# Product-key top-k of a mixture layer: the gather block's first level moved behind the gate build, softmax exponential ahead of the index decoding

## Chip, cores and metric

One core of one Trainium2 chip runs the whole kernel in one launch. The metric is the device time of one execution in microseconds (us); the kernel is run several times and the median is taken.

## What is computed

A hybrid decoder layer for 512 tokens of width 1024: latent attention and retention side by side, one output projection, then a product-key mixture (PEER) with 128 x 128 experts, each a single neuron, and a final norm. The change lies in the mixture alone. Cut to it, the reference is:

```python
q = (xt @ w_query).reshape(T, 8, 2, 128)               # 8 heads, 2 halves
s = einsum('thpd,pkd->thpk', q, sub_keys)              # 128 scores per half
s_top, i_top = top_k(s, 16)                            # first level
cand = s_top[:, :, 0, :, None] + s_top[:, :, 1, None]  # 16 x 16 sums
best, pos = top_k(cand.reshape(T, 8, 256), 16)         # second level
eidx = take(i_top[:, :, 0] * 128 + i_top[:, :, 1], pos)
g = softmax(best)                                      # gates, 16 a head
a = gelu(einsum('thkd,td->thk', expert_u[eidx], x))
out = einsum('thk,thkd->td', g * a, expert_v[eidx])
```

So every token takes 8 x 16 = 128 experts out of 16384.

## The kernel before

The 512 tokens are four blocks of 128. Blocks 0 to 2 (`DB`) are computed densely: a gate matrix with one column for every expert, mostly zeros, multiplies the activations of all experts. The experts come in 128 chunks of 128. For each chunk c a **U chunk** (`u_chunk`, L782) loads `raw` (L779, on the SP queue), splits it into a high part on ACT (L78) and a low part on POOL for the first 12 chunks and on DVE for the rest (L79), does 24 matmuls of 384 columns (L83 to L85), and applies Gelu on ACT (L794) into a buffer `ga` or `gb`. A **V chunk** (`v_load` L851, `v_mm` L872) loads `vraw` (L857), splits it on ACT and POOL into `vhi` and `vlo`, multiplies the activations with the gates (`wf`, L866; rounded copies `wh` L868 on ACT and `wl` L869 on DVE) and does 18 matmuls of 512 columns. `R0` is 36: 36 U chunks run ahead, so the V loop (L962) does V chunk c and U chunk c + 36 in each round. There are 37 activation buffers; chunk c + 37 takes that of chunk c, which is freed by `wf` of c. `raw` has three buffers, `vraw`, `hi`, `lo`, `vhi`, `vlo`, `wf`, `wh` and `wl` two each, the gates `gtl` three.

Block 3 (`GB`) is computed by gathers: 128 indirect transfers (L883, issued by POOL) fetch the chosen rows of the U table, DVE takes the dot products (L891), and 128 more fetch rows of the V table, which DVE sums (L904). They need the expert indices `eidx`, and run beside the dense loops of V and U chunks.

**Queries and top-k.** `query` (L554) computes, for groups of blocks and heads, the queries, and `scores` (L561) the 128 scores of each half, which ACT copies out of PSUM (L567) into the block's score tile `blk`. `Q0` and `Q1` do heads 0 and 1 of blocks 0, 1 and 2, 3; `Q2` and `Q3` heads 2 to 7 of all four. Behind each head, `level1` (L616) calls `topk16` for each half. It is eight values at a time on DVE:

```python
V.max(vals[:, 0:8], src)                              # L601
V.max_index(idx[:, 0:8], vals[:, 0:8], src)           # L602
V.match_replace(src, vals[:, 0:8], src, -BIG)         # L603
V.max(vals[:, 8:16], src)                             # L604
V.max_index(idx[:, 8:16], vals[:, 8:16], src)         # L605
```

The values of blocks 0 and 1 go to a tile `fhi`, of block 2 to `flo`, of block 3 to `v`. `level2` (L637) forms the 50 sums of a head that can be among the best 16 (L645 to L651) and calls `topk16` on them; it is called for half of the heads at a time, for blocks 0 to 2 first in the middle of the queries. `topk` (L655) decodes the positions into the two index halves with comparisons and trees of additions on DVE (L660 to L690), and takes the best value off the scores (L687 to L689). `gates` (L693) applies Exp on ACT (L697), normalises on DVE, splits the gates of blocks 0 to 2 into a high and a low half (L708 to L710), and for block 3 writes `eidx` (L704, L705). `topk_fin` (L712) transposes a block's indices and gates on TensorE (L717) and copies them to half precision on ACT (L721); it may not be issued ahead of the matmuls of the last U chunk written before it. How many those are by blocks 0, 1 and 2 is the table `UF`.

**Gate build.** `g_steps` (L812) has 48 steps, spread over the U chunks up to the 32nd. Each makes four one-hot arrays on DVE (L823 to L826, three buffers `ohs`), 16 short matmuls (L832, L833), ACT copies into `stg` (two buffers, L836), and a transfer to the gate matrix `Gd` in DRAM (L840), from which the V loop loads it (`gtl`, L848). The last one-hot is kept as `last["o"]`, and the last four U chunks ahead of the V loop are held until it is issued. The memory of the one-hots and of `stg` is that of the front stage, which holds the score tiles of blocks 0 to 2.

**Start of the gathers.** In round `LEAD` = 2 of the V loop (L963), not to be issued ahead of `last["o"]`, come the second level, decoding and gates of block 3. Then `h2n` is loaded (L972), the normalised input of block 3, into memory that was the top-k stage's, and from there on POOL runs in the order in which the program is written: the split `vlo` of a V chunk, then the gathers of that round (2.56 a round on average, later 1.12), beginning with round 2.

What sets the order on the other engines is a scheduler: it goes through the program, and puts instructions that it holds ready ahead of others that wait; within an engine the order is then fixed. Up to L771 the SP queue is by hand, behind it the scheduler's too.

Of the kernel before, what the change touches and what calls it, by code (L numbers as in the profile page):

```python
# [8 lines left out]
F32 = mybir.dt.float32  # L9
# [5 lines left out]
AF = mybir.ActivationFunctionType  # L15
# [6 lines left out]
H = 8  # L22
# [7 lines left out]
GB = 3  # L30
# [6 lines left out]
GPU = 2  # L37
HOLD = 4
NPL = 12
UF = {0: 2, 1: 7, 2: 12}  # L40
QS = (((0, 1), (0, 1)), ((2, 3), (0, 1)), ((0, 1, 2, 3), (2, 3, 4)), ((0, 1, 2, 3), (5, 6, 7)))
LEAD = 2
GSC = float(2 ** 14)
# [7 lines left out]
def build(ctx: ExitStack, tc: tile.TileContext, A, out):  # L51
    nc = tc.nc
    V, S, P, T, G = nc.vector, nc.scalar, nc.gpsimd, nc.tensor, nc.sync
# [6 lines left out]
    def acc():  # L60
        return ps.tile([128, 512], F32, name="acc", bufs=3)

    def tpb():
        return ps.tile([128, 512], F32, name="tp", bufs=2)

    def ab():
        return ps.tile([128, 512], F32, name="ab", bufs=2)
# [4 lines left out]
    def raw_t():  # L72
        return st.tile([128, 1024], F32, name="raw", bufs=3)
# [15 lines left out]
    tk = ptk.enter_context(tc.tile_pool(name="topk", bufs=1, side="right", reuse_waits="tile"))  # L89
# [20 lines left out]
    for hf in range(2):  # L110
        p = tpb()
# [442 lines left out]
    def query(bs, hs):  # L554
        n = len(bs) * 128
        for b in bs:
            Sc[b] = blk[b].rearrange("p a c -> p (a c)").rearrange("p (h q k) -> p h q k", h=8, q=2)
        pend = []

        def scores():  # L560
            qs, h, q = pend.pop()  # L561
            p4 = acc()
            for i in range(len(bs)):
                cs = slice(i * 128, (i + 1) * 128)
                T.matmul(p4[:, cs], qs[:, cs], subk[:, q, :], start=True, stop=True)
            for i, b in enumerate(bs):
                last["qa"] = S.activation(Sc[b][:, h, q], p4[:, i * 128:(i + 1) * 128], AF.Copy).ins  # L567
            if q:
                for b in bs:
                    level1(b, h)  # L570
                if h == H // 2 - 1:
                    for b in DB:
                        level2(b, 0)

        for h in hs:
            for q in range(2):
                raw = raw_t()
                G.dma_start(raw, A["w_query"][2 * h + q])
                hi, lo = split(raw, P)
                pa = ab()  # L580
                for k in range(8):
                    ks = slice(k * 128, (k + 1) * 128)
                    mm3(pa[:, :n], hi[:, ks], lo[:, ks], hh[:, bs[0]:bs[0] + len(bs), k, :],
                        hl[:, bs[0]:bs[0] + len(bs), k, :], k == 0, k == 7)
                qs = w2()
                S.activation(qs[:, :n], pa[:, :n], AF.Copy)
                if pend:
                    scores()
                pend.append((qs, h, q))
        scores()  # L590
# [23 lines left out]
    lv, tin = {}, {}  # L614

    def level1(b, h):  # L616
        if b not in lv:
            if b == 1:
                t = lv[0][2]
            else:  # L620
                t = (tk if b == GB else fr).tile([128, 512 if b == GB else 1024], F32,
                                                 name=("fhi", None, "flo", "v1")[b], bufs=1)
            o = 512 * (b == 1)
            v = t[:, o:o + 256].rearrange("p (h q a) -> p h q a", h=8, q=2)
            i = t[:, o + 256:o + 512].bitcast(U32).rearrange("p (h q a) -> p h q a", h=8, q=2)
            lv[b] = v, i, t
        v1, i1, _ = lv[b]
        for q in range(2):
            topk16(v1[:, h, q, :], i1[:, h, q, :], Sc[b][:, h, q, :], 128)

    def spare(b):
        f = blk[b].rearrange("p a c -> p (a c)")
        return (f[:, 0:128].rearrange("p (h k) -> p h k", h=8),
                f[:, 128:256].bitcast(U32).rearrange("p (h k) -> p h k", h=8),
                f[:, 256:256 + H * NC_].rearrange("p (h n) -> p h n", h=8), f[:, 1024:1536])
# [17 lines left out]
            topk16(bst[:, h], bpos[:, h], cd[:, h], NC_)  # L653

    def topk(b):  # L655
        bst, bpos, _, ti = spare(b)
        i1 = lv[b][1]
        di = tk.tile([128, 2, 17, 8], F16, name="di", bufs=1)
        V.memset(di[:, :, 0, :], 0.0)
        V.tensor_copy(di[:, :, 1:, :], i1.rearrange("p h q a -> p q a h"))  # L660
        dd = tk.tile([128, 2, 16, 8], F16, name="dd", bufs=1)
        V.tensor_sub(dd, di[:, :, 1:, :], di[:, :, :16, :])
        ij = tk.tile([128, 2, 16, 8], F16, name="ij", bufs=1)
        ph = tk.tile([128, 16, 8], F16, name="ph", bufs=1)
        V.tensor_copy(ph, bpos.rearrange("p h k -> p k h"))
        full = [128, 16, 16, 8]

        def t4k():
            return tk.tile([128, 16, 16, 8], F16, name="t4k", bufs=2)

        ge, tm = t4k(), t4k()
        V.tensor_tensor(ge, ph[:, None].to_broadcast(full), kc[:, 0, :, None, :].to_broadcast(full), op=OP.is_ge)
        V.tensor_mul(tm, ge, dd[:, 0, :, None, :].to_broadcast(full))
        tree(ij[:, 0], tm, V)
        V.tensor_mul(ge, ge, kc[:, 1, :, None, :].to_broadcast(full))
        pb = tk.tile([128, 16, 8], F16, name="pb", bufs=1)
        tree(pb, ge, V)
        V.tensor_sub(pb, ph, pb)
        tm = t4k()
        V.tensor_tensor(tm, pb[:, None].to_broadcast(full), kc[:, 2, :, None, :].to_broadcast(full), op=OP.is_ge)  # L680
        V.tensor_mul(tm, tm, dd[:, 1, :, None, :].to_broadcast(full))
        tree(ij[:, 1], tm, V)
        if b == 2:
            ti = tk.tile([128, 512], F32, name="t4k", bufs=2)
        ti = ti.rearrange("p (q s) -> p q s", q=4)
        nm = tk.tile([128, 8], F32, name="nmx", bufs=1)
        V.tensor_copy(nm, bst[:, :, 0])  # L687
        ee = ti[:, 3].rearrange("p (h k) -> p h k", h=8)
        V.tensor_sub(ee, bst, nm[:, :, None].to_broadcast([128, 8, 16]))  # L689
        V.tensor_copy(ti[:, :2], ij.rearrange("p q k h -> p q (k h)"))  # L690
        tin[b] = ti

    def gates(b, after=None):  # L693
        ti = tin[b]
        ee = ti[:, 3].rearrange("p (h k) -> p h k", h=8)
        with tc.issue_after(after) if after else ExitStack():
            S.activation(ee, ee, AF.Exp)  # L697
        se = tk.tile([128, 8], F32, name="se", bufs=1)
        V.reduce_sum(se, ee, axis=AX.X)
        V.reciprocal(se, se)  # L700
        gg = gsm if b == GB else ti[:, 2]
        V.tensor_mul(gg.rearrange("p (k h) -> p h k", h=8), ee, se[:, :, None].to_broadcast([128, 8, 16]))
        if b == GB:
            V.scalar_tensor_tensor(ti[:, 2], ti[:, 0], 128.0, ti[:, 1], op0=OP.mult, op1=OP.add)  # L704
            V.tensor_copy(eidx, ti[:, 2])  # L705
            return
        gh = tk.tile([128, 16, 8], F16, name="pb", bufs=1).rearrange("p k h -> p (k h)")
        V.tensor_scalar(gh, gg, GSC, None, op0=OP.mult)  # L708
        V.scalar_tensor_tensor(ti[:, 3], gg, GSC, gh, op0=OP.mult, op1=OP.subtract)
        V.tensor_copy(ti[:, 2], gh)  # L710
# [16 lines left out]
    last = {}  # L727
# [69 lines left out]
    nu = 0  # L797
    for b in DB:
        level2(b, 1)
        topk(b)  # L800
        gates(b, last["qa"])
        while nu < UF[b]:
            u_chunk(nu, P if nu < NPL else V)
            nu += 1
        topk_fin(b, last["u"])
# [156 lines left out]
    for c in range(NK - LB):  # L962
        if c == LEAD:  # L963
            with tc.issue_after(last["o"]):
                level2(GB, 0)
                level2(GB, 1)
                topk(GB)
                gates(GB)
            ptk.close()
            lg = ctx.enter_context(tc.tile_pool(name="gside", bufs=1, side="right", reuse_waits="tile"))  # L970
            h2n = lg.tile([128, 1024], F32, name="h2n")
            G.dma_start(h2n, h2d)  # L972
            asl = lg.tile([128, 128], F32, name="asl")
            wsl = lg.tile([128, 128], F32, name="wsl")
            ga_it = gather_steps(h2n, asl, wsl)
            ctx.enter_context(tc.manual_schedule(engines={mybir.EngineType.Pool}))
        w = v_load(c)
        for d in range(ND):
            v_mm(c, w, d)
        if c + R0 < NK:  # L980
            u_chunk(c + R0, V)
        if c < LEAD:
            continue
        credit += CR[0] if c + R0 < NK else CR[1]
        while credit >= 1:
            credit -= 1
            next(ga_it, None)
# [89 lines left out]
```

## Time and profile before

| | us |
|---|---|
| median of 3 runs | 1591.3 |
| lowest, highest | 1589.39, 1597.22 |
| the profiled execution | 1585.5 |
| its span | 1583.7 |
| PE (TensorE) busy | 1507.8, 95% |
| DVE busy | 1276.3, 81% |
| POOL busy | 824.2, 52% |
| ACT busy | 622.1, 39% |

The span is what the profiler saw, from the first instruction to the last; the execution's own time is a little longer. Busy times are of one engine each and overlap. PE is the TensorE matmul queue; SP is the queue that issues most transfers. PEclk is the share of full clock that TensorE was granted. In a timeline, "x2" means two instructions put together in a row, and a bracket tells how long the engine was idle before and what ended that.

### The profile page before, as it was taken

What the parts mean: (1) busy time and instruction counts of PE and PEld (TensorE: products, weight loads), DVE (VectorE), ACT (ScalarE), POOL (GpSimd) and SP (SyncE); (2) the same over time, 40 slices, a digit from 0 to 9 for tenths busy, and PEclk for the clock granted to TensorE, in tenths of its full rate; (3) what the DMA queues carried; (4) which work ended last, traced back from release to release, by engine and by line L of the source; (5) the groups of instructions that cost most, each with busy time, mean ns of one, the idle gap of its engine ahead of it and who ended that gap; (6) DMA issues with size and microseconds to landing.
All of it is one profiled execution on the core that took longest, in us unless ns stands there. A gap on an engine that the chain in (4) does not pass through costs nothing.

```text
span 1583.7 us, 23659 instructions
## 1 busy us (share of the span) xinstructions
PE 1507.8 (95%) x8692; PEld 1358.3 (86%) x8692; DVE 1276.3 (81%) x2369; ACT 622.1 (39%) x1027; POOL 824.2 (52%) x490
## 2 busy tenths in 40 slices
PE   7899999899969997999999999999999999999997
PEld 6788988688969996899999999999999999997885
DVE  6876754768999999989978877888887877889953
ACT  4433244443334555533333333333333333333432
POOL 0332651743440000167877767777777777767413
PEclk9999999999989999999999999999999999999998
DMA  9455350542232787989888998899888899899941
GB/s 359 181 173 185 128 179 9 191 133 82 85 102 80 222 259 225 309 298 343 312 306 312 336 332 301 297 318 354 297 313 313 298 335 329 297 337 354 318 158 70
DMA packets 194310, 389.29 MB, mean 246 GB/s; under 512 B 12049, under 2 KB 111377, under 8 KB 194194
## 3 DMA queue, kind: packets, MB, share of 16 engines
q1 hardware_dynamic: 156178, 250.93, 46.8%
q0 software_dynamic: 36864, 134.23, 23.6%
q10 hardware_dynamic: 1152, 2.62, 0.4%
q8 instruction: 68, 1.11, 0.3%
q14 instruction: 48, 0.39, 0.1%
HBM read 357.86 MB, written 29.88 MB: 245 GB/s over the span
## 4 chain that ended last, share of the span: by engine, by line
PE 49%; DMA 16%; DVE 15%; issue 12%; POOL 8%; ACT 1%; SPq 0%; POOLq 0%; DVEq 0%; ACTq 0%
DMA grow<-in_expert_v_dram,eidx 8%; PE ab L85 6%; PE ab L83 6%; PE ab L84 6%; PE acc L83 5%; PE acc L85 5%; PE acc L84 5%; POOL grow L883 4%; DMA vraw<-in_expert_v_dram 4%; PE tp L85 2%; PE tp L84 2%; PE tp L83 2%; POOL vlo L79 2%; PE ob L85 1%; PE ob L84 1%
## 5 line engine op out<-in xcount | busy, mean ns | idle before, releaser
L83 PE MATMUL ab<-hh,hi 128*128 128x384 f32 (+2 forms) x1184 | 404.4, 342 | 7.0 <-ACT ga L794 6.5
L85 PE MATMUL ab<-hh,lo 128*128 128x384 f32 (+2 forms) x1184 | 403.8, 341 | 2.8 <-POOL lo L79 2.0
L84 PE MATMUL ab<-hl,hi 128*128 128x384 f32 (+2 forms) x1184 | 401.8, 339 | 0.0
L79 POOL TENSOR_TENSOR vlo<-vraw,vhi 128x1024 fp32r<-128x1024 f32 x92 | 239.2, 2600 | 291.8 <-ACT vhi L78 291.0
L78 ACT ACTIVATE hi<-raw 128x1024 fp32r<-128x1024 f32 x192 | 203.7, 1061 | 405.5 <-PE ab L84 245.6
L891 DVE SCALAR_TENSOR_TENSOR junk<-grow,h2n 128x1024 bf16<-128x1024 f32 x128 | 193.2, 1509 | 64.2 <-DMA grow<-in_expert_u_dram,eidx 63.3
L79 DVE TENSOR_TENSOR lo<-raw,hi 128x1024 fp32r<-128x1024 f32 x147 | 212.3, 1445 | 32.9 <-ACT hi L78 32.8
L83 PEld LDWEIGHTS ab<-hh,hi 128*128 128x128 f32 x1184 | 224.1, 189 | 15.1 <-ACT ga L794 7.2
L904 DVE SCALAR_TENSOR_TENSOR gacc<-grow,wsl,gacc 128x1024 f32<-128x1024 f32 x126 | 186.8, 1490 | 61.3 <-DMA grow<-in_expert_v_dram,eidx 61.0
L85 PEld LDWEIGHTS ab<-hh,lo 128*128 128x128 f32 x1184 | 223.8, 189 | 8.0 <-POOL lo L79 2.4
L84 PEld LDWEIGHTS ab<-hl,hi 128*128 128x128 f32 x1184 | 224.0, 189 | 7.1
L883 POOL DMA_INDIRECT grow<-in_expert_v_dram,eidx x128 | 192.9, 1507 | 50.2 <-DVE gacc L904 22.2
L883 POOL DMA_INDIRECT grow<-in_expert_u_dram,eidx x128 | 177.5, 1387 | 50.4 <-DVE junk L891 21.7
L79 POOL TENSOR_TENSOR lo<-raw,hi 128x1024 fp32r<-128x1024 f32 x45 | 110.5, 2456 | 146.9 <-ACT hi L78 146.8
L868 ACT ACTIVATE wh<-wf 128x384 fp32r<-128x384 f32 x110 | 57.6, 524 | 258.3 <-issue 230.2
L84 PE MATMUL acc<-vlo,wh 128*128 128x512 f32 x330 | 128.9, 391 | 0.0
L85 PE MATMUL acc<-vhi,wl 128*128 128x512 f32 x330 | 128.5, 391 | 0.4 <-DVE wl L869 0.4
L78 ACT ACTIVATE vhi<-vraw 128x1024 fp32r<-128x1024 f32 x110 | 115.3, 1048 | 34.1 <-DMA vraw<-in_expert_v_dram 33.9
L83 PE MATMUL acc<-vhi,wh 128*128 128x512 f32 x330 | 128.5, 390 | 0.0
L869 DVE TENSOR_TENSOR wl<-wf,wh 128x384 fp32r<-128x384 f32 x110 | 89.6, 814 | 13.2 <-ACT wh L868 12.0
L83 PE MATMUL acc<-hi,hh 128*128 128x256 f32 (+2 forms) x296 | 91.9, 318 | 6.9 <-ACT hi L78 4.8
L84 PE MATMUL acc<-lo,hh 128*128 128x256 f32 (+2 forms) x296 | 93.8, 317 | 1.5 <-DVE lo L79 0.8
(365 smaller groups left out, 2924.6 us busy)
## 6 DMA issues: line engine op xcount, KB each, us to landing
raw<-in_uT_dram SPq DMA_DIRECT2D x128, 512.0 KB
vraw<-in_expert_v_dram SPq DMA_DIRECT2D x110, 512.0 KB
Gd<-stg SPq DMA_DIRECT2D x12, 2048.0 KB
gtl<-Gd SPq DMA_DIRECT2D x32, 768.0 KB
raw<-in_wadaT_dram SPq DMA_DIRECT2D x40, 512.0 KB
raw<-in_w_query_dram SPq DMA_DIRECT2D x20, 512.0 KB
raw<-in_expert_v_dram SPq DMA_DIRECT2D x18, 512.0 KB
raw<-in_w_out_dram SPq DMA_DIRECT2D x16, 512.0 KB
```

The costliest lines, as they stand in the source:

```text
L78: S.activation(hi[:, :n], raw[:, :n], AF.Copy)
L79: lo_engine.tensor_sub(lo[:, :n], raw[:, :n], hi[:, :n].bitcast(F32))
L83: T.matmul(o, wh, rh, start=start, stop=False, skip_group_check=skip)
L84: T.matmul(o, wh, rl, start=False, stop=False, skip_group_check=skip)
L85: return T.matmul(o, wl, rh, start=False, stop=stop, skip_group_check=skip)
L868: S.activation(wh, wf, AF.Copy)
L869: V.tensor_sub(wl, wf, wh.bitcast(F32))
L883: P.indirect_dma_start(out=r, out_offset=None, in_=A[table], in_offset=bass.IndirectOffsetOnAxis(ap=eidx[:, s:s + 1], axis=0))
L891: V.scalar_tensor_tensor(jk, r, 1.0, h2n, op0=OP.mult, op1=OP.mult, accum_out=asl[:, s:s + 1])
L904: V.scalar_tensor_tensor(g, r, wsl[:, s:s + 1], g, op0=OP.mult, op1=OP.add)
```

## The change

It does three things. The first-level top-k of block 3 is taken out of `query`, and all eight heads of it are called in round `LEAD` of the V loop, behind the same condition as the second level and in front of it. The largest value, the subtraction and Exp come out of `topk` and `gates` into a function `soft`, called ahead of `topk`; with it block 2's indices and gates no longer get a tile of their own (`t4k`), but lie in the score tile of the block, as those of the others do. And `UF` is larger by one for each block, so that the transposes of each block come one U chunk later in the program. No operation is added or left out.

```diff
@@ -37,7 +37,7 @@
 GPU = 2
 HOLD = 4
 NPL = 12
-UF = {0: 2, 1: 7, 2: 12}
+UF = {0: 3, 1: 8, 2: 13}
 QS = (((0, 1), (0, 1)), ((2, 3), (0, 1)), ((0, 1, 2, 3), (2, 3, 4)), ((0, 1, 2, 3), (5, 6, 7)))
 LEAD = 2
 GSC = float(2 ** 14)
@@ -567,7 +567,8 @@
                 last["qa"] = S.activation(Sc[b][:, h, q], p4[:, i * 128:(i + 1) * 128], AF.Copy).ins
             if q:
                 for b in bs:
-                    level1(b, h)
+                    if b != GB:
+                        level1(b, h)
                 if h == H // 2 - 1:
                     for b in DB:
                         level2(b, 0)
@@ -653,7 +654,7 @@
             topk16(bst[:, h], bpos[:, h], cd[:, h], NC_)
 
     def topk(b):
-        bst, bpos, _, ti = spare(b)
+        _, bpos, _, _ = spare(b)
         i1 = lv[b][1]
         di = tk.tile([128, 2, 17, 8], F16, name="di", bufs=1)
         V.memset(di[:, :, 0, :], 0.0)
@@ -680,21 +681,22 @@
         V.tensor_tensor(tm, pb[:, None].to_broadcast(full), kc[:, 2, :, None, :].to_broadcast(full), op=OP.is_ge)
         V.tensor_mul(tm, tm, dd[:, 1, :, None, :].to_broadcast(full))
         tree(ij[:, 1], tm, V)
-        if b == 2:
-            ti = tk.tile([128, 512], F32, name="t4k", bufs=2)
+        V.tensor_copy(tin[b][:, :2], ij.rearrange("p q k h -> p q (k h)"))
+
+    def soft(b, after=None):
+        bst, _, _, ti = spare(b)
         ti = ti.rearrange("p (q s) -> p q s", q=4)
         nm = tk.tile([128, 8], F32, name="nmx", bufs=1)
         V.tensor_copy(nm, bst[:, :, 0])
         ee = ti[:, 3].rearrange("p (h k) -> p h k", h=8)
         V.tensor_sub(ee, bst, nm[:, :, None].to_broadcast([128, 8, 16]))
-        V.tensor_copy(ti[:, :2], ij.rearrange("p q k h -> p q (k h)"))
         tin[b] = ti
-
-    def gates(b, after=None):
+        with tc.issue_after(after) if after else ExitStack():
+            S.activation(ee, ee, AF.Exp)
+
+    def gates(b):
         ti = tin[b]
         ee = ti[:, 3].rearrange("p (h k) -> p h k", h=8)
-        with tc.issue_after(after) if after else ExitStack():
-            S.activation(ee, ee, AF.Exp)
         se = tk.tile([128, 8], F32, name="se", bufs=1)
         V.reduce_sum(se, ee, axis=AX.X)
         V.reciprocal(se, se)
@@ -797,8 +799,9 @@
     nu = 0
     for b in DB:
         level2(b, 1)
+        soft(b, last["qa"])
         topk(b)
-        gates(b, last["qa"])
+        gates(b)
         while nu < UF[b]:
             u_chunk(nu, P if nu < NPL else V)
             nu += 1
@@ -962,8 +965,11 @@
     for c in range(NK - LB):
         if c == LEAD:
             with tc.issue_after(last["o"]):
+                for h in range(H):
+                    level1(GB, h)
                 level2(GB, 0)
                 level2(GB, 1)
+                soft(GB)
                 topk(GB)
                 gates(GB)
             ptk.close()
```

## Rows read from the trace of the kernel before

**Rows 1.** The page's first line: the span of the profiled execution.

```profile
span 1583.7 us, 23659 instructions
```

**Rows 2.** Table by stretch, core 0: us, busy us (instructions) of each engine, PEclk, DMA share, GB/s.

```profile
376.00:427.00 51.00, 51.00 (x265) 43.97 (x264) 50.06 (x364) 18.72 (x54) 20.01 (x9) 1.00 0.25 84
427.00:501.00 74.00, 60.26 (x323) 59.06 (x322) 73.52 (x244) 29.39 (x39) 25.18 (x10) 0.91 0.28 87
501.00:644.00 143.00, 129.10 (x1196) 118.91 (x1195) 138.89 (x221) 77.93 (x135) 0.00 (x0) 0.95 0.77 226
645.00:683.00 38.00, 37.17 (x199) 34.19 (x198) 36.37 (x124) 18.46 (x26) 9.03 (x4) 1.00 0.97 305
453.00:469.00 16.00, 15.50 (x74) 14.98 (x72) 15.90 (x24) 7.56 (x10) 8.12 (x4) 0.82 0.34 106
700.00:800.00 100.00, 100.00 (x510) 91.31 (x510) 93.95 (x109) 35.61 (x49) 77.67 (x46) 1.00 0.91 328
```

**Rows 3.** Chain of waits from 420 to 700 us: start, us, engine or DMA, line.

```profile
645.12 9.71 DMA Gd<-stg
```

**Rows 4.** Timeline of DVE, last one-hot to `eidx`: start us, us, engine, line, operation.

```profile
642.68 0.68 DVE L826 TENSOR_TENSOR ohs<-ohs,gt 128x1024 f16<-128x1024 f16 x1
...
645.55 0.58 DVE L645 TENSOR_TENSOR blk<-v 128x64 f32<-128x64 f32 x5
...
682.15 0.23 DVE L705 CAST eidx<-blk 128x128 int32<-128x128 f32 x1
```

**Rows 5.** Timeline of DVE, first MAX8 of the last two sets of scores.

```profile
423.61 0.47 DVE L601 MAX8 fhi<-blk 128x8 f32<-128x128 f32 x2
...
428.29 0.47 DVE L601 MAX8 fhi<-blk 128x8 f32<-128x128 f32 x2
```

**Rows 6.** Groups of DVE instructions from 376.9 to 430 us (`v`: the gather block's).

```profile
L601 DVE MAX8 v<-blk 128x8 f32<-128x128 f32 x9 | 2.4, 275 | 0.0
```

**Rows 7.** Timeline of ACT, the last evacuation of scores.

```profile
426.12 0.76 ACT L567 ACTIVATE blk<-acc 128x128 f32<-128x128 f32 x4
```

**Rows 8.** Timeline of PE, the wait behind the first Exp; in brackets: idle before.

```profile
452.46 0.69 PE L83 MATMUL ab<-hh,hi 128*128 128x384 f32 x1 [5.52 <-ACT ga L794]
```

**Rows 9.** Groups of DVE instructions from 427 to 501 us, L708.

```profile
L708 DVE TENSOR_SCALAR pb<-blk 128x128 f16<-128x128 f32 x2 | 4.8, 2392 | 0.0
```

**Rows 10.** Timeline of DVE, the last write of block 2's gate tile.

```profile
519.54 0.22 DVE L710 CAST t4k<-pb 128x128 f32<-128x128 f16 x1
```

**Rows 11.** Timeline of PE, the last two transposes of block 2.

```profile
521.73 0.39 PE L717 MATMUL ob<-ident,t4k 128*128 128x128 f32 x2
```

**Rows 12.** Timeline of PE, first matmul of U38 and of V3.

```profile
684.00 0.34 PE L83 MATMUL ab<-hh,hi 128*128 128x384 f32 x1
...
688.16 0.39 PE L83 MATMUL acc<-vhi,wh 128*128 128x512 f32 x1
```

**Rows 13.** Timeline of POOL, first gather and split of V3.

```profile
682.68 1.23 POOL L883 DMA_INDIRECT grow<-in_expert_u_dram,eidx  x1 [4.77 <-DVE eidx L705]
...
685.41 2.41 POOL L79 TENSOR_TENSOR vlo<-vraw,vhi 128x1024 fp32r<-128x1024 f32 x1
```

**Rows 14.** Timeline of the SP queue, `h2n` and the first U load behind it.

```profile
682.46 0.33 SPq L972 DMA_DIRECT2D h2n<-h2d  x1
...
688.23 0.42 SPq L779 DMA_DIRECT2D raw<-in_uT_dram  x1
```

**Rows 15.** Timeline of ACT, Exp of the gather block.

```profile
656.75 0.31 ACT L697 ACTIVATE blk<-blk 128x128 f32<-128x128 f32 x1
```

**Rows 16.** Groups of DVE instructions from 645 to 683 us.

```profile
L79 DVE TENSOR_TENSOR lo<-raw,hi 128x1024 fp32r<-128x1024 f32 x6 | 8.7, 1443 | 1.4 <-ACT hi L78 1.4
...
L866 DVE TENSOR_TENSOR wf<-ga,gtl 128x384 f32<-128x384 f32 x6 | 3.1, 552 | 0.0
```

**Rows 17.** Line L779 from 0 to 700 us: duration min/median/max, first and last start.

```profile
L779 SPq DMA_DIRECT2D raw<-in_uT_dram x44: 327/328/6546, 398.0 to 695.5; - x44
```

**Rows 18.** Groups of DVE instructions from 300 to 427 us, second-level FIND_INDEX8.

```profile
L605 DVE FIND_INDEX8 blk<-blk 128x8 uint32<-128x50 f32 x12 | 2.3, 202 | 0.0
```


## Prediction

> **What bounds the kernel now.** I read the page's first part, then the table by stretch, the chain of waits, and the timelines of the engines around the places that the diff touches. The profiled execution took 1585.5 us, of which the span is 1583.7 [rows 1]; the median of the runs is 1591.3, 5.8 above it. Differences below are worked out on the profiled execution and added to the median; 0.5% of it, about what a measurement of this kernel can tell from no change, is 8 us.
>
> The table by stretch [rows 2] shows two limits, one after the other. From 376 to 644 us DVE is busy 50.1 of 51, 73.5 of 74 and 138.9 of 143 us, while TensorE idles 13.7 us in the second stretch and 13.9 in the third: DVE sets the pace, and work there is worth its own length. From 700 on TensorE is busy 100 of 100 us, at full clock: whatever delays its V and U matmuls comes out at the end, and DVE work costs nothing unless TensorE waits for it. The chain of waits joins the two stages: the last gate copy, its transfer `Gd` (9.71 us) [rows 3], then the first V load. So the end is O, the end of the last one-hot on DVE (643.4 us [rows 4]), plus a fixed rest, as long as TensorE stays fed behind it. I need two numbers: how far O moves, and what TensorE loses after it.
>
> **Part 1: first-level top-k of the gather block leaves the queries.** 16 calls of topk16 leave. Price of one: a set of four (one for each block) begins at 423.61 and the next at 428.29 [rows 5], so 4.68 / 4 = 1.17 us. Nine of the 16 run in the dense stretch [rows 6]; the other seven are ahead of it and taken as free. 9 x 1.17 = 10.5 us of dense DVE time. But that is not the gain. DVE would then run ahead of the queries, and TensorE, busy 51 of 51 us in 376 to 427 [rows 2], does not deliver scores sooner. The last set of scores is evacuated by ACT from 426.12, 0.76 us for four blocks [rows 7], so the first is there at about 426.4; DVE took the set up at 428.29. It gains 428.29 − 426.4 = 1.9 us, and 1.17 for its own call in that set: O comes **3.1 us earlier**. Bounds 1.9 and 10.5; I take 3.1, because the index decoding behind it needs all eight heads.
>
> **Part 2: softmax exponential ahead of the index decoding, one tile less.** No operation is added. Today ACT waits at Exp behind DVE, and the Gelu behind it lets TensorE idle 5.52 us at 452.46 [rows 8]; that goes, but TensorE's idle time in these stretches is covered by DVE: 0. What the reordering can do to DVE is to shift which two-input operations fall into POOL's subtractions: L708 took 2.39 us for 128x128 elements, twice, L710 with as many 0.22 [rows 9, 10], so a collision more or less is worth ±2.2 us. There are as many of either as before, so I take 0 and keep ±2.2 for the range. New is that block 2's gate tile lies in its score tile, which the one-hot stage's memory waits for; the tile is free only after the transposes. From the last write of that tile at 519.54 to the end of the transposes at 521.73 + 0.39 = 522.1 it is 2.6 us [rows 10, 11]. Bounds 0 and 2.6; I take **+1**.
>
> **Part 3: transposes one U chunk later.** Block 2's wait for DVE today, not for the chunk: they end 2.6 us behind that write [rows 10, 11]. The chunk that moves in front brings its load on SP and its split on ACT and POOL or DVE; there are as many of them as before. Price if the chunk does bind: one U chunk, 688.16 − 684.00 = 4.16 us of TensorE [rows 12], and TensorE has 13.9 us idle beside DVE in that stretch: 0.
>
> **Part 4: the 16 calls arrive behind O.** 16 x 1.17 = 18.8 us are put in front of the second level, which starts at 645.55 today and ends with `eidx` at 682.38 [rows 4], that is O + 39.0. DVE is busy 36.4 of 38 us there [rows 2], so the calls find no hole. What waits: POOL runs in written order here and waited 4.77 us for `eidx`; then come two gathers and only then the split of V3 (685.41 + 2.41 = 687.82), and TensorE starts V3 at 688.16 [rows 12, 13]. So today the path has 0.34 us of slack at V3. On the SP queue `h2n` waits for the same `eidx` (682.46), and loads are behind it [rows 14]. On ACT the block's Exp runs at 656.75 today [rows 15]; the calls make it 18.8 us later, and splits, Gelus and `wh` copies stand behind it. ACT is busy 18.5 of 38 us there [rows 2], so its delay alone costs 0 as long as it isn't ordered ahead of the covering chunks' work.
>
> With the change V3 is ready 18.8 us later, or up to 24.6 if four more splits of 1.44 us [rows 16] are taken in between: four of the covering chunks need theirs before that. Beside it TensorE can do U chunks: six products wf(0) to wf(5) are done by 683 [rows 16], and chunk c+37 takes the buffer freed by wf(c), so U39 to U42 are free to run and U43 after wf(6), which waits for nothing of V3: 5 x 4.16 = 20.8 us. TensorE then idles between 18.8 − 0.34 − 20.8, that is 0, and 24.6 − 0.34 − 20.8 = 3.5 us. I take the upper end, since the splits must run first to give that cover, and half a microsecond of queueing: **+4**.
>
> The row of 453 to 469, behind the 5.52 us idle, shows a granted clock of 0.82 [rows 2]: 16 x 0.18 = 2.9 us of matmul time lost behind one idle stretch, the higher level being 2.4 GHz and the lower 1.2. The Trainium skill, "TensorE: Matmul & The Clock Gate", section "Part 1: The HAM clock gate", says that the throttled state is the default and that activity releases it; by that rule the wait at V3 costs more than its length, and the sum would be 2.9 us higher. The sum here goes without it, since 4 us spread over several chunks need not be one idle stretch; 2.9 stays in the range.
>
> **Sum:** −3.1 + 0 + 1 + 4 = +1.9 us, so 1591.3 + 1.9 = 1593.2, **1593**: no change that can be told. Its own range runs from −3.1 − 2.2 = −5 to −1.9 + 2.2 + 2.6 + 4 + 2.9 = +10.
>
> **Rivals.**
> *The cover fails (slower).* Place: V3's wait on TensorE. It decides when fewer U chunks than five stand in front of V3 in TensorE's order, or when their loads stand behind `h2n` on SP: 44 U loads had been issued by 695.5, two of them, at 688.23 and at 695.5, behind `h2n`, so 42 (U0 to U41) before `h2n` [rows 14, 17]. If SP keeps that order, three chunks cover (U39 to U41): TensorE idles 18.5 to 24.3 − 12.5 = 6 to 12 us; the middle, 9, gives −3.1 + 1 + 9 + 2.9 (clock) = +10, **1601**. With no cover it is −3.1 + 18.5 + 2.9 = +18, 1610. Over 0.5% from an idle time of 10.1 on, less what the clock takes. For it: 0.34 us of slack now, POOL in a fixed order, and today V3 follows U38, as the program writes it [rows 12]. Against it: the scheduler orders what is ready, and may put U chunks and loads in front.
>
> *The dense stretch gives all back (faster).* If the second level of blocks 0 to 2 fills the time until the last scores, the whole 10.5 us come off O; with full cover and no hold the time is 1591.3 − 10.5 = **1581**, with a loss of 3 us at V3 1584. Against it: all 12 calls of the second level's first half are done by 427 us [rows 18], and the other half needs the last scores.
>
> *The change doesn't reach the bound.* DVE collisions and holds eat the 3.1 us, and V3 is covered in full: **1591**. For it: both terms are no larger than a collision.
>
> **How the numbers follow.** Forecast 0.52, cover fails 0.30, faster 0.13, no effect 0.05. Faster by over 0.5%: the faster rival and 0.02 for scatter, 0.15. Slower: the cover rival, nearly all of it, and 0.05 of the forecast's upper tail, 0.34. The rest, 0.51, is within 0.5%. The range goes from 1584, the upper part of the faster rival, to 1608, most of the slower one; what is left out is half of the faster (0.07) and the end of the slower (0.08).
>
> **What would show it.** Right: the last one-hot ends 1 to 5 us before 643.4; no first-level call on tile `v` before it, 16 behind; `eidx` some 58 to 64 us behind O; U39 to U43 on TensorE between V2 and V3; idle time in front of V3 under 5 us; Exp no longer in front of a Gelu that TensorE waits for. Wrong: V3 directly behind U38 with a wait of 12 us or more for POOL's `vlo` and a granted clock below 1.00 behind it; `raw` loads issued in one bunch behind `h2n`; or the last one-hot 8 us or more earlier, with TensorE fed throughout.

## Result and profile after

The changed kernel takes 1609.0 us (median of 4 runs, 1606.5 to 1610.3) against 1593.8 for the kernel before (4 runs): the ratio is 1.0091, with a 95% interval of 1.0066 to 1.0116. By that ratio it is about 14.5 us slower; the medians lie 15.2 apart. The forecast was 1593 and no difference that can be told, in a range of 1584 to 1608. The result lies just above the range, on the side of the first rival, though, as it turns out, not by that rival's way.

The first line of the profile's page after, and the table by stretch with the columns of [rows 2]:

```profile
span 1604.8 us, 23653 instructions
```
```profile
376.00:427.00 51.00, 51.00 (x262) 43.66 (x261) 42.23 (x309) 17.71 (x48) 19.43 (x8) 1.00 0.26 82
427.00:501.00 74.00, 61.84 (x333) 60.07 (x333) 72.60 (x237) 28.98 (x43) 25.91 (x10) 0.91 0.29 93
501.00:644.00 143.00, 129.10 (x1173) 119.50 (x1172) 136.11 (x214) 75.90 (x131) 0.00 (x0) 0.94 0.74 220
644.00:683.00 39.00, 35.71 (x200) 32.94 (x199) 38.94 (x167) 15.75 (x24) 8.08 (x3) 0.92 0.95 293
...
700.00:800.00 100.00, 94.80 (x466) 83.08 (x466) 88.09 (x104) 32.86 (x44) 73.09 (x44) 1.00 0.87 308
800.00:900.00 100.00, 98.83 (x499) 89.13 (x498) 90.67 (x106) 36.15 (x51) 83.43 (x48) 1.00 0.94 332
```

DVE lost 7.8 us of its work in the first stretch (50.06 to 42.23), as the moved calls should take away, and it bought nothing: from the last scores to the last one-hot it took 217.8 us, where it had been 217.7 (table below). The new thing is the row of 700 to 800: TensorE was busy 100 us of 100 with 510 matmuls [rows 2], and is now busy 94.8 with 466.

The chain behind the gate build, on DVE and POOL (timelines, start and duration in us):

```profile
645.25 0.70 DVE L829 TENSOR_TENSOR ohs<-ohs,gt 128x1024 f16<-128x1024 f16 x1
...
648.12 1.07 DVE L602 MAX8 v<-blk 128x8 f32<-128x128 f32 x5
```
```profile
708.44 0.23 DVE L707 CAST eidx<-blk 128x128 int32<-128x128 f32 x1
```
```profile
709.61 1.26 POOL L886 DMA_INDIRECT grow<-in_expert_u_dram,eidx  x1 [26.97 <-DVE eidx L707]
711.17 0.94 POOL L886 DMA_INDIRECT grow<-in_expert_u_dram,eidx  x1 [0.30 <-PE ab L85]
712.14 2.41 POOL L79 TENSOR_TENSOR vlo<-vraw,vhi 128x1024 fp32r<-128x1024 f32 x1
...
719.85 2.55 POOL L79 TENSOR_TENSOR vlo<-vraw,vhi 128x1024 fp32r<-128x1024 f32 x1
```

The last one-hot ends at 645.95 and `eidx` at 708.67: 62.7 us behind it, where the kernel before had 39.0 [rows 4]. POOL waits 27 us for it where it waited 4.8 [rows 13], and the split of V3, behind two gathers, is done at 714.55.

**Where the time went.** To see at what time TensorE falls behind I count the U and V matmuls that it has begun, at 24 a U chunk (4.16 us) and 18 a V chunk (4.09 us), in both traces, and take the difference as a lag behind the profiled execution of before. That execution was a quick one (1585.5, where the runs of before in these measurements have medians of 1594 to 1596), so kernels with before's time show a lag of some 4 to 6 us; what tells is where a lag grows. The table has, for each kernel of this study, the time from the last matmul that makes scores to the end of the last one-hot, and the growth of the lag, beyond that of the last one-hot itself, in four parts (one trace of each kernel):

| kernel | last scores to last one-hot | to 700 us | 700 to 900 | 900 to 1400 | 1400 to 1550 |
|---|---|---|---|---|---|
| before | 217.7 | 0 | 0 | 0 | 0 |
| changed | 217.8 | 4.1 | 10.5 | −0.2 | 4.1 |
| level 1 back | 219.5 | 0.8 | 0.2 | −0.2 | 0.0 |
| level 1 alone | 216.3 | 6.6 | 5.6 | −0.1 | 1.9 |
| changed, gathers from round 5 | 217.5 | 4.4 | 5.0 | −0.3 | 2.5 |
| before, gathers from round 5 | 217.5 | 1.1 | 0.0 | 0.0 | 0.9 |
| changed, gathers from round 8 | 217.9 | 4.1 | 1.6 | 0.3 | 3.3 |
| changed, thin start | 217.8 | 4.5 | 6.8 | 9.4 | 7.6 |
| last head alone | 216.3 | 0.7 | 0.1 | −0.1 | 2.4 |
| changed, own tile | 216.4 | 4.0 | 11.7 | 0.8 | 6.7 |
| changed, late chain | 217.9 | 4.1 | 2.1 | 8.4 | 3.9 |
| level 1 alone, late chain | 216.3 | 5.9 | 0.0 | 4.5 | 7.0 |
| changed, no cover (680 for 700) | 217.9 | 4.1 | 19.6 | −0.1 | 5.2 |

For the changed kernel: nothing up to the last one-hot, some 3 us more than in kernels without the move up to 700, 10.5 between 700 and 900, and some 3 more at the end of the U chunks (the three kernels at before's time that have no move of all heads stand at 0.7 to 1.1, 0 to 0.2, and 0 to 2.4 there). 16 to 17 together, beside the 14.5 of the ratio.

### The profile page after: what moved, and what is told of

It reads as the page before. It is cut to its first block, busy times and chain, and to the rows that moved or that the text cites. A ratio compares the mean times of both kernels' runs of the same rounds, so it can differ in the third digit from the quotient of the medians.

```text
span 1604.8 us, 23653 instructions
## 1 busy us (share of the span) xinstructions
PE 1520.1 (95%) x8692; PEld 1365.6 (85%) x8692; DVE 1283.5 (80%) x2369; ACT 620.5 (39%) x1025; POOL 819.3 (51%) x490
## 4 chain that ended last, share of the span: by engine, by line
PE 32%; issue 20%; DMA 19%; POOL 14%; DVE 13%; ACT 1%; SPq 0%; POOLq 0%; DVEq 0%; ACTq 0%
POOL grow L886 9%; DMA grow<-in_expert_v_dram,eidx 8%; DMA grow<-in_expert_u_dram,eidx 5%; POOL vlo L79 4%; PE ab L85 4%; PE ab L83 4%; PE ab L84 4%; PE acc L83 3%; PE acc L84 3%; PE acc L85 3%; DMA vraw<-in_expert_v_dram 2%; DVE lo L79 1%; PE ob L485 1%; PE tp L83 1%; PE tp L84 1%
## 5 line engine op out<-in xcount | busy, mean ns | idle before, releaser
L894 DVE SCALAR_TENSOR_TENSOR junk<-grow,h2n 128x1024 bf16<-128x1024 f32 x128 | 185.3, 1448 | 57.4 <-DMA grow<-in_expert_u_dram,eidx 56.5
L79 DVE TENSOR_TENSOR lo<-raw,hi 128x1024 fp32r<-128x1024 f32 x147 | 197.2, 1342 | 31.0 <-ACT hi L78 30.9
L83 PE MATMUL acc<-vhi,wh 128*128 128x512 f32 x330 | 123.5, 391 | 0.6 <-ACT wh L871 0.5
```

The source lines that it names most:

```text
L79: lo_engine.tensor_sub(lo[:, :n], raw[:, :n], hi[:, :n].bitcast(F32))
L83: T.matmul(o, wh, rh, start=start, stop=False, skip_group_check=skip)
L894: V.scalar_tensor_tensor(jk, r, 1.0, h2n, op0=OP.mult, op1=OP.mult, accum_out=asl[:, s:s + 1])
```

## Experiments

Each ratio is to the kernel before, measured beside it (medians 1595.6 for experiments 1 to 4, 1595.5 for 5 to 8, 1595.3 for 9 to 11), with its 95% interval in brackets.

**1. The first level put back.** The changed kernel with `level1` of all blocks in the queries again:

```diff
-                    if b != GB:
-                        level1(b, h)
+                    level1(b, h)
...
-                for h in range(H):
-                    level1(GB, h)
```

> The changed kernel with the gather block's first level put back into the queries; the earlier exponential, the dropped tile and the later transposes stay. If the loss comes from the moved calls (my theory), the time goes back to that of the kernel before: 1590 to 1598 us, ratio 0.997 to 1.003. If it comes from the other parts (one-hots held until the transposes of block 2, U chunks moved), it stays at 1603 to 1612.

Measured: 1594.8, ratio 1.0003 (0.9987 to 1.0020). The earlier Exp, the dropped tile and the later transposes together cost nothing that can be told in the time, though the last one-hot comes 1.8 us later against the scores (219.5 for 217.7). Without the moved calls there is no loss.

**2. The first level alone.** The same edit made to the kernel before, the other way round.

> The kernel before with the first-level move alone. My theory: the whole loss is here, 1603 to 1612 us, with `eidx` some 26 us later behind the last one-hot than before and TensorE's lag growing between 700 and 900 us. If the parts add up, this and the run with the first level put back make the changed kernel's difference between them (about +15 us). The rival (the other parts cost it): 1590 to 1598.

Measured: 1603.2, ratio 1.0053 (1.0034 to 1.0071). Slower, and at the lower edge of the forecast, 8.4 us of the 14.5. So the parts do not simply add up: the others cost nothing alone, and some 6 us on top of the move. The table puts most of the difference between 700 and 900 us (5.6 against 10.5). What in the order of the two kernels makes this difference was not settled.

**3 and 4. The gathers later.** One line, in the changed kernel and, as a control, in the kernel before:

```diff
-        if c < LEAD:
+        if c < LEAD + 3:
             continue
```

> The changed kernel, but POOL's gathers begin three rounds later (round 5 in place of 2), so that the splits of V3, V4 and V5 no longer stand behind `eidx` in POOL's written order. Nothing else changes. Theory one (V3 behind `eidx`; the covering U chunks are only borrowed, and V rounds then come at POOL's pace): the lag that grows by 10 us between 700 and 900 goes away, 1596 to 1601 us. Theory two (the 18.8 us of DVE work behind the gate build starve the splits of U chunks, whatever POOL does): no gain, 1605 to 1612.

> Control: the kernel before with the same later begin of the gathers. V3 had 0.34 us of slack there, so nothing is to be had at V3; the gathers have some 10 spare places in the loop and lose 7.7 of them. Expected 1590 to 1597 us, ratio 0.998 to 1.003. If it gains as much as the changed kernel does by the same edit, the edit helps by something other than the wait of V3.

Measured: 1601.4, ratio 1.0035 (1.0019 to 1.0051), 0.4 us above what theory one allows: of the 14.5 us, 9 come back, where 8 to 13 were expected. The control: 1591.1, ratio 0.9978 (0.9957 to 1.0000), a gain of at most 0.4%. By the times alone the two gains (0.56% and 0.22%) are hardly apart, given their intervals. The table parts them: between 700 and 900 the growth falls from 10.5 to 5.0 in the changed kernel, and is 0 in the control with and without the edit. So taking V3 to V5 out from behind `eidx` does a part of what theory one says. The waits of TensorE in that stretch show the larger part of what is left (engine, what it waited for, us, times, longest):

```profile
PE ab L85 <- DVE lo L79: 2.9, 2, 2.5
```

It is a U chunk's split, late on DVE. DVE had stood idle ahead of the first product with gathered rows until `h2n` had landed, and came to the split of the chunk that waits 2.5 us only at 735.62, behind further products (timeline of DVE):

```profile
723.41 1.23 DVE L894 SCALAR_TENSOR_TENSOR junk<-grow,h2n 128x1024 bf16<-128x1024 f32 x1 [6.70 <-DMA h2n<-h2d]
...
735.62 1.22 DVE L79 TENSOR_TENSOR lo<-raw,hi 128x1024 fp32r<-128x1024 f32 x1
```

The products stand in DVE's fixed order. That the order was made for an earlier arrival is a reading of this, which experiment 5 tries.

**5. The gathers later still.** The changed kernel, `LEAD + 6`, and `CR = (2.7, 1.12)`.

> The changed kernel with the gathers begun in round 8 in place of 2, and 2.70 in place of 2.56 of them a round so that they still fit. `eidx` came about 64 to 69 us behind the last one-hot in the runs so far; V8 is due about 83 us behind it. If the rest of the loss (5 us between 720 and 740 in the run with round 5) is TensorE waiting because DVE or POOL stands at the first gathers, which the fixed order expects earlier, it goes too: 1595 to 1599 us, and the lag does not grow between 700 and 900. Rival (the 18.8 us of DVE work cost what they cost): 1600 to 1604, as with round 5. A thicker gather stream could add some us at the end of the loop.

Measured: 1599.9, ratio 1.0025 (1.0008 to 1.0043). The time lies between the two forecasts, next to the rival's. By stretches the theory holds: the growth between 700 and 900 is 1.6 in place of 10.5, and of 5.0 with round 5. The rest is what is lost ahead of 700 and at the end of the U chunks, 3.3 there.

**6. A thin start of the gathers.** To see whether V rounds behind the wait are paced by POOL:

```diff
-        credit += CR[0] if c + R0 < NK else CR[1]
+        credit += (1.5 if c < LEAD + 20 else 2.85) if c + R0 < NK else CR[1]
```

> The changed kernel, gathers begun in round 2 as written, but only 1.5 a round in rounds 2 to 21 and 2.85 from then on. V3 waits for `eidx` as before, and TensorE runs the same U chunks ahead. If the 10 us lost between 700 and 900 come from the V rounds behind that wait running at POOL's pace (7.4 us a round in the trace, while TensorE has V chunks of 4.1 us left to do), POOL's round falls to about 5.5 us and 5 to 9 of the 10 us come back: 1600 to 1604 us. If they come from DVE or from the order of TensorE's queue, nothing comes back: 1606 to 1612.

Measured: 1614.7, ratio 1.0115 (1.0090 to 1.0140): a miss by the time, outside both forecasts. The edit itself cost more than it gave: with 2.85 gathers a round TensorE loses 9.4 us between 900 and 1400 and 7.6 behind it. But between 700 and 900 the growth is 6.8 in place of 10.5. The waits of TensorE from 700 to 900 us, in the changed kernel and, in the second fence, in this one:

```profile
PE acc L84 <- POOL vlo L79: 4.8, 8, 1.1
PE ab L85 <- DVE lo L79: 1.4, 2, 0.7
```
```profile
PE acc L83 <- ACT vhi L78: 2.9, 1, 2.9
PE ab L85 <- DVE lo L79: 1.5, 2, 0.8
PE acc L85 <- DVE wl L872: 0.8, 1, 0.8
```

The waits for POOL's `vlo` are gone, and the V chunks do follow each other faster: from V3 to V8 the first matmul that needs `vlo` comes every 6.3 us (714.07 to 745.32), where it came every 7.5 in the changed kernel (714.96 to 752.43). But only 3.7 of the 10.5 us come back, where 5 to 9 were expected: other steps of the V path, the load with its high part (`vhi`) and `wl`, now hold TensorE for another 3.7 us. So POOL's pace was a part of the loss, and other steps of the V path stand close behind it.

**7. The last head alone.** The kernel before, gathers from round 5 as in experiment 4, and only head 7 of the gather block's first level (2 of 16 calls) moved behind the gate build:

```diff
                 for b in bs:
-                    level1(b, h)
+                    if b != GB or h != H - 1:
+                        level1(b, h)
...
             with tc.issue_after(last["o"]):
+                level1(GB, H - 1)
                 level2(GB, 0)
```

> The kernel before with the first level of the gather block moved for its last head alone (2 of 16 calls, 2.3 us), and the gathers begun in round 5. The calls that DVE does beside the waits for scores stay there; the two that stand behind the last scores go. Theory: the last one-hot comes some 1 to 3 us earlier against the last scores, and 2.3 us more behind it cost nothing with the later gathers: 1587 to 1592 us, ratio 0.995 to 0.998. Rival: the shift of collisions on DVE eats it, 1591 to 1596.

Measured: 1592.3, ratio 0.9984 (0.9969 to 0.9999). That is 0.3 us above the theory's range and inside the rival's. It is the fastest form of the idea, and no faster than the control with no move. But the column up to the last one-hot is worth a look: 216.3, the same 1.4 us as with all 16 calls moved in experiment 2. All that the move has to give at the dense stretch is in the last head.

**8. A tile of its own for block 2.** In the changed kernel:

```diff
         bst, _, _, ti = spare(b)
+        if b == 2:
+            ti = tk.tile([128, 512], F32, name="ti2", bufs=1)
```

> The changed kernel with a tile of its own for block 2's indices and gates, so that the one-hots don't wait for its transposes. In the changed kernel DVE went without other work from 504.2 to 507.3 us but for one split of 1.2: about 2 us should come back, the last one-hot 2 us earlier against the last scores: 1605 to 1608 us. If the one-hots were not held by that tile, nothing changes.

Measured: 1608.7, ratio 1.0086 (1.0064 to 1.0109), 0.7 above the forecast, and no difference that can be told from the changed kernel. The step itself is right: the last one-hot comes 1.4 us earlier against the scores (216.4 for 217.8). That is the price of the hold. By the table it is lost again behind the last one-hot (11.7 for 10.5 and 6.7 for 4.1).

**9 and 10. The whole chain later.** The changed kernel, and the kernel of experiment 2, with

```diff
-LEAD = 2
+LEAD = 7
...
-CR = (2.56, 1.12)
+CR = (2.8, 1.12)
...
-        if c < LEAD:
+        if c < LEAD + 3:
```

> The changed kernel with the whole chain of the gather block (first level, second level, decoding, gates) in round 7 of the V loop in place of 2, gathers from round 10 and 2.8 a round. The splits of the U chunks behind the gate build then come ahead of the chain on DVE. Theory: two parts of the loss go, the wait for a split at about 657 to 659 us with the lower clock around it (3.3 us between the last one-hot and 700 us more than in the kernels without the move) and the 10 us between 700 and 900: 1593 to 1598 us. Rival (DVE has no room for the chain anywhere, U splits wait elsewhere): 1599 to 1606.

> The kernel before with the first-level move alone, and the chain and the gathers as late as in the run before this one. The move alone brought the last one-hot 1.4 us nearer to the last scores than before; if nothing behind it is lost any more, this is 1 to 2 us faster than the kernel before: 1591 to 1596 us. If the late begin costs at the end of the loop (a thicker gather stream), 1597 to 1603.

Measured: 1604.9, ratio 1.0067 (1.0043 to 1.0090), and 1600.3, ratio 1.0044 (1.0021 to 1.0067): both forecasts of the theory missed, and both times lie in the ranges of their rivals. Between 700 and 900 the growth is 2.1 and 0.0, as expected. But the loss ahead of 700 stays: although the chain stands five rounds later in the program, the scheduler puts it where it was, right behind the last one-hot. The timeline of DVE in experiment 9:

```profile
646.54 2.35 DVE L79 TENSOR_TENSOR lo<-raw,hi 128x1024 fp32r<-128x1024 f32 x2
...
648.81 2.80 DVE L602 MAX8 v<-blk 128x8 f32<-128x128 f32 x14
...
658.83 1.21 DVE L79 TENSOR_TENSOR lo<-raw,hi 128x1024 fp32r<-128x1024 f32 x1
```

And what the later begin gives between 700 and 900 is lost again: 12.3 us behind 900 in experiment 9, 11.5 in 10, against 3.9 and 1.8 in the kernels that they start from. In experiment 9 the waits of TensorE from 900 to 1390 us are for the splits of U chunks on DVE:

```profile
PE ab L85 <- DVE lo L79: 5.3, 3, 3.2
```

Experiment 10 has 2.5 us of them there, experiment 6 had 6.7, and the changed kernel and experiment 5 have none. This goes with the denser stream of gathers, whose products DVE takes. That the density does it, and not the late begin, is suggested by experiments 5 (late, 2.7 a round, no such loss) and 6 (begun in round 2, then 2.85, the same loss); no run changes the density alone.

**11. No cover.** The U chunks of rounds 3 to 7 may not be issued ahead of the V matmuls of their own round:

```diff
         if c + R0 < NK:
-            u_chunk(c + R0, V)
+            with tc.issue_after(last["v"]) if 3 <= c < 8 else ExitStack():
+                u_chunk(c + R0, V)
```

(`last["v"]` is the last matmul of `v_mm`.)

> The changed kernel, but the U chunks of rounds 3 to 7 may not be issued ahead of the V matmuls of their own round, so that none of them covers the wait of V3. Theory (the covering chunks are borrowed: V4 to V7 have none of their own left behind the wait, and the V path gives one round in some 7.4 us): TensorE idles 17 to 22 us ahead of V3, but the lag does not grow by 10 us between 720 and 900; the whole loss is only 6 to 12 us larger than in the changed kernel, 1614 to 1621 us. Rival (the chunks cover for good, and the 10 us behind them have another cause): the idle time is added in full, 1626 to 1632 us.

Measured: 1616.1, ratio 1.0133 (1.0099 to 1.0168), as the theory has it. The timeline of TensorE at V3, and the table by stretch around it:

```profile
711.40 0.80 PE L84 MATMUL acc<-vlo,wh 128*128 128x512 f32 x1 [16.92 <-POOL vlo L79]
```
```profile
676.00:693.00 17.00, 17.00 (x89) 15.56 (x88) 16.97 (x89) 8.66 (x12) 2.40 (x1) 1.00 0.48 148
693.00:710.00 17.00, 1.48 (x7) 0.89 (x5) 12.21 (x25) 2.83 (x3) 3.14 (x3) 0.69 0.35 108
710.00:717.00 7.00, 5.60 (x15) 4.49 (x16) 2.47 (x4) 0.45 (x2) 6.21 (x5) 0.53 0.91 326
717.00:720.00 3.00, 3.00 (x19) 3.00 (x19) 2.46 (x4) 1.03 (x2) 2.56 (x2) 1.00 0.84 249
```

TensorE idles 16.9 us and then does 15 matmuls at a granted clock of 0.53, near the lower level of 1.2 GHz, before it is back at full clock: 19.6 us of lag from 680 to 900, the 2.7 beyond the idle time put down to the clock. Behind that the lag does not grow by anything up to 1400. In the changed kernel TensorE works through that wait but for 1.4 us, and loses some 9 more afterwards, 10.5 together. Between the two lies what the cover is worth: 9 of 20 us.

## Why the prediction was wrong

**The step that failed** is in part 4: "Beside it TensorE can do U chunks: ... 5 x 4.16 = 20.8 us. TensorE then idles between ... 0, and ... 3.5 us." The wait came as worked out (V3's split is done 714.55 − 645.95 = 68.6 us behind the last one-hot, 44.5 before [rows 4, 13]: 24.1 us later, where 18.8 to 24.6 were forecast), and the cover all but held. In the trace after, behind six matmuls of V3 that need no `vlo` (694.98 to 696.5), TensorE does four U chunks, 96 matmuls, in one run to 715.1, with two waits of 0.7 us for their splits. Four chunks did where five were counted, because TensorE came to V3 4.2 us later behind the last one-hot than before (49.0 us, 44.8 before) and had those six matmuls, 1.4 us, to do first: 4.2 + 1.4 + 4 x 4.16 + 1.4 of idle time are 23.6 of the 24.1 us. What was wrong is that this cover was taken as free. It is a loan. There are 37 activation buffers, so U chunks can run only a few ahead (by the code; no run changed their number). At V3 TensorE is four U chunks ahead of the order before, at V13 one: behind the wait it does ten V chunks with only seven U chunks between them, and V chunks follow each other no faster than their path (load, two splits, products, two buffers for each) lets them. In the trace POOL's `vlo` begins at 712.14 for V3 and at 719.85 for V4, and some 7.4 us apart on the mean up to 794, where a V chunk takes TensorE 4.09. The same 75 us from V3 on, groups of PE instructions, the changed kernel first (714.9 to 790), then the kernel before (688.1 to 763):

```profile
L85 PE MATMUL ab<-hh,lo 128*128 128x384 f32 x57 | 19.2, 336 | 0.0
...
L84 PE MATMUL acc<-vlo,wh 128*128 128x512 f32 x30 | 12.4, 414 | 2.6 <-POOL vlo L79 2.5
```
```profile
L85 PE MATMUL ab<-hh,lo 128*128 128x384 f32 x73 | 24.5, 336 | 0.0
L84 PE MATMUL acc<-vlo,wh 128*128 128x512 f32 x28 | 11.0, 391 | 0.0
```

The V chunks go on at the same rate (30 and 28 matmuls of this form), but there are 16 fewer of the eight U matmuls of this form a chunk: two U chunks, 8.3 us, not done. Experiment 11 shows it from the other side: without the loan nothing is paid back. So the idle time ahead of V3, which I priced at 4, is 1.4 us, and the term that belonged in its place, with what is paid back, is 10.5. It is not the whole miss: against the sum the front is 2.2 us off, this term 6.5, and two costs of some 3 each are not in it.

**The front of DVE** (−3.1 and +1, together −2.1) came out at +0.1. The moved calls gave 1.4 us (experiments 2 and 7) in place of 3.1. The first set of last scores was indeed taken up at once, with 1.0 us of waiting ahead of it:

```profile
428.85 0.49 DVE L602 MAX8 fhi<-blk 128x8 f32<-128x128 f32 x2 [1.02 <-ACT blk L567]
```

so DVE was ahead there as predicted; the rest was lost between there and the last one-hot. No run took that apart, but the waits of DVE in that stretch grew. What it waited for, us, times and longest, from the first of the last scores to the last one-hot, in the changed kernel (428.85 to 645.95) and then in the kernel before (428.29 to 643.36):

```profile
DVE lo L79 <- ACT hi L78: 3.5, 3, 2.0
DVE ohs L826 <- PE tp L836: 3.2, 6, 1.3
```
```profile
DVE lo L79 <- ACT hi L78: 2.0, 2, 1.3
DVE ohs L823 <- PE tp L833: 1.9, 4, 0.7
```

The longest, 2.0 us, is the one that goes with the tile in experiment 8; the others show that DVE, with less to do, waited more for ACT and TensorE, so that work taken off it there was not worth its own length. The hold of the one-hots cost 1.4 (experiment 8) where I took 1. That the whole 10.5 us of dense work would not come off the bound, the argument against the second rival, was right. The wait of TensorE behind the first Exp, which part 2 has go, did not (6.3 us for a Gelu between 427 and 501, 5.5 before [rows 8]); as part 2 priced it at 0, the sum does not change. (L708, which part 2 counts among the two-input operations, has one tensor input; its row shows the stretch all the same.)

**Missing altogether** is a cost of 3 us ahead of 700. The calls stand in one block in front of the split of a U chunk, which was ready on ACT at 653.4, and TensorE waited 2.4 us for it; the granted clock between 644 and 683 was 0.92, where it had been 1.00 before [rows 2]. The timelines of TensorE and DVE:

```profile
659.41 0.45 PE L85 MATMUL ab<-hh,lo 128*128 128x384 f32 x1 [2.37 <-DVE lo L79]
```
```profile
658.13 1.23 DVE L79 TENSOR_TENSOR lo<-raw,hi 128x1024 fp32r<-128x1024 f32 x1
```

I had priced the splits as a delay to `eidx`, not `eidx`'s chain as a delay to the splits. No run has the split first: experiment 9 was meant to, and did not move it. With the move alone (experiment 2) the loss ahead of 700 is 6.6, and TensorE's wait there is another one, 4.5 us for the V side's `wh`: what the block holds up depends on the order around it.

**Still open** are the 3 us at the end of the U chunks: TensorE waits there 4.3 us once for the V side's `wh`, 1.7 with the first level put back, 1.9 in the kernel before. In the table this column is between 1.9 and 7.6 in all the kernels with all calls moved and between 0 and 2.4 in the others. No run tells what makes it. Open too is why the other parts of the change, which cost no time by themselves, make the move dearer.

**Rivals.** "The cover fails" gave a time near the result, 1601 to 1610, for a reason that did not occur: neither TensorE's order nor the loads behind `h2n` held the U chunks back (45 U loads were issued ahead of `h2n`, 42 before). Its price for no cover at all, +18, stands beside the +20.9 of experiment 11 against before, which has the other 3 to 6 us too. Its clock term of 2.9, from one row, stands beside the 2.7 of experiment 11. The sentence from the Trainium skill, "TensorE: Matmul & The Clock Gate", section "Part 1: The HAM clock gate", that the slow state is the default, agrees with the row of 0.53 behind the 16.9 us; in the changed kernel it played no part at V3, since TensorE idled there for two times 0.7 us only, and the granted clock from 683 to 720 was 1.00. The third rival, that the change does not reach the bound, was right about the front, where the gain was eaten (+0.1), and wrong in that a wait that is covered costs nothing.

## What to carry to other kernels

Work that one engine does ahead of its turn to cover a wait may be borrowed, here where a ring of buffers bounds how far it can run ahead: price what the late path must do afterwards without that partner, not just the wait. Here a V path late by 24.1 us cost 19.6 us without the cover and 10.5 with it; at some 7.4 us a chunk beside a round of 8.25 it could win back less than 1 us a round. Before work is moved off a dense stretch, ask which of its instructions stand behind the last input: here two of sixteen calls held all the gain, 1.4 us, while moving the other fourteen gave nothing there, and all sixteen were in the way where they went.

## What was not expected of the hardware

Two things of the fixed orders rather than of the engines. A chain written five rounds later in the program was put at the same place in DVE's order (experiment 9). And a later or thinner begin of the gathers, with more of them a round behind it, cost 4.5 to 9.4 us of TensorE's time between 900 and 1400 at 2.8 to 2.85 a round, and nothing that can be told at 2.56 to 2.7: the stream had less room than DVE's busy share of 88 to 94% between 700 and 900 in the rows suggests.
